# A second Strassen level for the products 0 and 1 of seven convolution pairs, with h's quarter sums prepared in v's stage

## The chip, the cores and the metric

The kernel runs on one core of a Trainium2 chip. A core has TensorE (matrix products; PE in the profile, and PEld for its weight loads), VectorE (DVE), ScalarE (ACT), GpSimd (POOL) and SyncE (SP, which here issues almost all DMAs). The metric is the device time of one execution in microseconds, the median of several runs.

## What is computed

One layer of a decoder trunk over 1024 positions of width 1024, in float32. After a norm, h is multiplied by one wide weight matrix, and the columns feed a gated linear attention and a short gated convolution; the two are merged, projected, gated once more and normed.

```python
h = rms_norm(x, norm_mix_g[i])
proj = jnp.einsum('bsd,dc->bsc', h, w_in[i])
(q, k, v, z_a, gk_low, cb, cc, xc, z_c, g_a, g_c) = jnp.split(proj, idx, axis=-1)
...
u = causal_dwconv(cc * xc, conv_w[i])
y_c = jnp.einsum('bsc,cd->bsd', (cb * u) * jax.nn.silu(z_c), w_branch_c[i])
```

`causal_dwconv` adds, for every channel, the values of a position and of the two before it, each times its own weight. The change lies in the four products cb, cc, xc and z_c (1024 columns each) and in this convolution.

## The kernel before

**Products.** Every matrix is cut into halves in both directions, and each product of 2x2 blocks is done by Strassen's scheme with seven block products instead of eight, numbered 0 to 6. Both operands of each are sums of blocks. A float32 value is split into a high part that the fast matmul form takes and a low part with the rest (`split`: a cast on ScalarE, a subtraction on VectorE), and a product is three matmuls: high x high, high x low, low x high (`mm3`). h's seven operands, high and low, are resident (`hres`). The weights' operands are made as they are needed in a ring of eight buffers (`RING`, tags whi and wlo): a load into raw, a sum into T, the split.

**Cells.** A `Cell` makes 256 columns of one projection for all positions: seven products of twelve matmuls of 512 columns each. Its partial results lie in three PSUM banks X, Y and V: product 0 goes to X and is copied to Y, product 1 to V, 2 adds onto Y, 3 onto X, 5 onto V, 4 and 6 onto Y. As soon as a quarter of the result is there, the cell's `cons` reads it from the bank. Two cells run in step as a pair (`pairs`), with the banks of one set each; the next pair uses the same six banks. In the convolution there are eight pairs, in this order: cc0 with xc0, zc0 with cb0, cc1 with xc1, and so on to zc3 with cb3. Four further cells, q0, k0, q1 and k1, run alone before them, and the gate cells (ga, gc) and the attention after them. v and z_a come first of all, by a function of their own (`wide`).

**Second level.** `Deep` takes product 0 of both cells of a pair, which have h's block in common, and does it again by Strassen's scheme: seven products of half size in both directions, 42 matmuls of 256 columns in place of 24 of 512. It runs in four steps (`run`, k from 0 to 3) that `line_up` puts between the last products of the pair before. Two more PSUM buffers (tag o: w and u) hold its partial results; ScalarE copies them on (into u, into the bank, and d into SBUF), and VectorE writes b's bank as u + d. Its h operands are quarter blocks of `hres[0]` and four sums of them, which `quarters` makes on VectorE during the first convolution pairs (t1 to t4; one of them overwrites a quarter of h itself, once product 0 of the second pair is done). In the kernel before, the six pairs from cc1 on have it.

**Order.** Nothing is issued as it is written. `Flow` records each operation, works out due times backwards from the order of the main matmuls, which is fixed, and then plans all five queues by a table of costs: of the operations that could start on an engine, the one that is due first. `nc.hurry` makes an operation due earlier by so many microseconds. `weave` spreads a generator's pieces over the ticks that the products give (two a product, one for each product of a second level). The engines then run the planned order as it stands.

**The convolution.** cc's results are copied into t (both halves of the positions, 1026 columns with two zeros ahead), xc's multiply them, and once both halves are there, three operations of 1024 columns make u. zc's sigmoid and product and then cb's results multiply u, half by half, and u is stored.

**Beside it.** `weights` prepares sums of blocks of the two last weight matrices for later (loads into wt, subtractions, stores to wtd), in eight pieces of 1 MB. The mask trim, the scratch tile junk and the identity are kept in SBUF from start to end.

Of the kernel before, what the change touches and what calls it, by code (L numbers as in the profile page):

```python
# [9 lines left out]
F32 = mybir.dt.float32  # L10
# [509 lines left out]
def kernel(  # L520
# [37 lines left out]
    ident = cp.tile([P, P], F32, name="ident")  # L558
    make_identity(tc.nc, ident.place())
    mhalf = cp.tile([P, 1], F32, name="mhalf")  # L560
    nc.gpsimd.memset(mhalf, -0.5)
    trim = cp.tile([P, P], I32, name="trim")
# [3 lines left out]
    junk = cp.tile([P, 512], BF16, name="junk")  # L566
# [11 lines left out]

    ped = [dram(f"ped{b}", D) for b in range(8)]
# [106 lines left out]
    def ring_steps(name, side, raw, fresh, mixed):  # L686
# [21 lines left out]
        if side == "A":  # L708
            a11, a21, a12, a22 = (r(n) for n in range(4))

            def s1():
# [3 lines left out]
                for kt in range(4):  # L715
# [5 lines left out]
                    lambda: put(a22())]  # L721
        b11, b12, b22, b21 = (r(n) for n in range(4))
        return [lambda: put(b11()), lambda: two("T1", b12, b11), lambda: two("T2", b22, k("T1")),
                lambda: put(b21()), lambda: two("T3", b22, b12), lambda: put(b22()),
                lambda: two("T4", b21, k("T2"), over="T2")]
# [5 lines left out]
    class Cell:  # L731
# [3 lines left out]
        def __init__(self, name, side, src, res, cons, prods=ORDER, begin=None, s1=None, u2=None, s5=None, fresh=(), mixed=False):  # L735
            self.name, self.side, self.src, self.res, self.cons = name, side, src, res, cons
            self.prods, self.begin, self.after = list(prods), begin, None
            self.get = {"u2": u2, "s5": s5}
            self.s1, self.seed, self.ready, self.halves = s1, None, lambda k: True, None
            self.raw, self.ring, self.order, self.Y, self.deep = [None] * 4, {}, None, None, None  # L740
            self.steps, self.fresh = ring_steps(name, side, self.raw, fresh, mixed), fresh
# [92 lines left out]
    class Deep:  # L834


        def __init__(self, pair, turned, pool):
            self.pair, self.turned, self.pool, self.ring = pair, turned, pool, []
            for c in pair:
                c.deep, c.prods = self, [k for k in c.prods if k]  # L840

        slots = 4
# [4 lines left out]
        def load(self, k):  # L847
            for c in self.pair:
                c.load(0)

        def prep(self, k):
# [3 lines left out]
            a, b = (c.raw[0] for c in self.pair)  # L855
            name = self.pair[0].name + self.pair[1].name
# [29 lines left out]
        def run(self, k):  # L886
            self.prep(k)
            a, b = self.pair
            left, right = slice(0, 256), slice(256, 512)
            if k == 0:  # L890
# [3 lines left out]
                self.u = pso.tile([P, 512], F32, tag="o", name=f"{a.name}u", bufs=2)  # L894
                a.X = bank(a, 0)
                nc.scalar.copy(self.u[:, left], self.w[:, left])
                nc.scalar.copy(a.X[:, left], self.w[:, left])
                self.d = self.pool.tile([P, 256], F32, tag="dw", name=f"{a.name}dw")
                nc.scalar.copy(self.d, self.w[:, right])
            elif k == 1:  # L900
                self.product(2, self.u[:, left], False)
                nc.scalar.copy(self.u[:, right], self.u[:, left])
                self.product(3, a.X[:, left], False)
            elif k == 2:
                self.product(4, self.u[:, right], False)
                nc.scalar.copy(a.X[:, right], self.u[:, right])
                b.X = bank(b, 0)
                tt(b.X.rearrange("p (n c) -> p n c", n=2), self.u.rearrange("p (n c) -> p n c", n=2),
                   self.d[:, None, :].to_broadcast([P, 2, 256]), op=ALU.add)
            else:  # L910
                self.product(5, a.X[:, right], False)
                self.product(6, b.X[:, left], False)
# [129 lines left out]
    with phase("prep0") as pool:  # L1042
        pr_ = slot(4, "h", "pTraw", (2, SEQ), F32)
# [31 lines left out]
        load(trim, tri)  # L1075
# [198 lines left out]
    with phase("v", [ph["prep0"]]) as qp:  # L1274
# [72 lines left out]
        weave(decays(0), 2)  # L1347
# [12 lines left out]
    with phase("qk", [ph["v"]]) as qp:  # L1360
# [65 lines left out]
        for g in range(4):  # L1426
            t, u = [], []

            def cc_begin(g=g, t=t, u=u):
                for j in range(2):  # L1430
                    t.append(vp.tile([P, SEQ + 2], F32, tag=f"t{j}", name=f"t{g}_{j}"))
                    u.append(vp.tile([P, SEQ], F32, tag=f"u{j}", name=f"u{g}_{j}"))
                    nc.gpsimd.memset(t[j][:, 0:2], 0.0)

            def cc_cons(i, j, src, t=t):
                nc.scalar.copy(t[j][:, 2 + i * HALF:2 + (i + 1) * HALF], src)

            done = {0: 0, 1: 0}

            def xc_cons(i, j, src, g=g, t=t, u=u, done=done):  # L1440
                ts = t[j][:, 2 + i * HALF:2 + (i + 1) * HALF]
                tt(ts, src, ts, op=ALU.mult)
                done[j] += 1
                if done[j] == 2:
                    k = 2 * g + j
                    nc.vector.tensor_scalar(u[j], t[j][:, 0:SEQ], cw[:, 0, k:k + 1], None, op0=ALU.mult)
                    stt(u[j], t[j][:, 1:SEQ + 1], cw[:, 1, k:k + 1], u[j], op0=ALU.mult, op1=ALU.add)
                    stt(u[j], t[j][:, 2:SEQ + 2], cw[:, 2, k:k + 1], u[j], op0=ALU.mult, op1=ALU.add)

            def zc_cons(i, j, src, g=g, u=u):  # L1450
                s = ev(f"s{g}_{i}_{j}")
                us = u[j][:, i * HALF:(i + 1) * HALF]
# [4 lines left out]
            def cb_cons(i, j, src, g=g, u=u):  # L1457
                k = 2 * g + j
                us = u[j][:, i * HALF:(i + 1) * HALF]
                tt(us, src, us, op=ALU.mult)  # L1460
                store(ud[i][k // 4][:, k % 4, :], us)

            for m, cons in (("cc", cc_cons), ("xc", xc_cons), ("zc", zc_cons), ("cb", cb_cons)):
                convs.append(Cell(f"{m}{g}", "B", W[f"{m}{g}"], hres, cons, begin=cc_begin if m == "cc" else None))
# [4 lines left out]
    with vp:  # L1469
        def weights(vp):  # L1470


            for w in range(2):
                for kt in range(4):
                    t = vp.tile([P, 4, 512], F32, tag="wt", name=f"wt{w}_{kt}", bufs=1)
                    load(t, wb[w][:, :, kt, :].rearrange("n p c -> p n c"))
                    yield 14
                    b11, b12, b22, b21 = (t[:, n] for n in range(4))
                    if w:
                        for n, q in enumerate((b11, b12, b22, b21)):  # L1480
                            k = kt + 4 * (n >= 2)
                            act(q, q, AF.Copy, scale=gple[:, k:k + 1])
                            if n != 1:
                                store(wtd[w][4 + (n + 1) // 2][:, kt, :], q)
                    tt(b11, b12, b11, op=ALU.subtract)
                    yield 2
                    tt(b12, b22, b12, op=ALU.subtract)
                    yield 2
                    tt(b22, b22, b11, op=ALU.subtract)
                    yield 2  # L1490
                    tt(b21, b21, b22, op=ALU.subtract)
                    for n, q in enumerate((b11, b22, b12, b21)):
                        store(wtd[w][n][:, kt, :], q)
                    yield 4
# [510 lines left out]
```

## Time and profile before

| | |
|---|---|
| median of 3 runs | 1077.94 us (1077.93 to 1078.25) |
| profiled execution | 1077.08 us, of which the span is 1075.3 us |
| granted TensorE clock | 0.998 of full speed |
| convolution stage (first cc0 matmul to the last cb3 one) | 311 to some 614 us |
| HBM | 158 MB read, 81 MB written, 222 GB/s over the span |

All instructions show the line of the planner's `emit` (L508), so the rows are told apart by tiles: cc1V is bank V of cell cc1, cc1w and cc1u are the second level's own buffers, cc1xc1S is a sum for it, turnedh one of h's quarter sums. Buffer numbers are left out. A row of the chain of waits is the time in which TensorE worked on that tile; x12 is one product of 512 columns.

### The profile page before, as it was taken

Reading aid. Unit: us, or ns where it says so; the run is one execution under the profiler, and the core shown is the slowest. Engines: PE = TensorE matmul, PEld = TensorE weight load, DVE = VectorE, ACT = ScalarE, POOL = GpSimd, SP = SyncE. Lnnn points to the kernel's source line nnn. Section 1 sums busy time; section 2 is a strip of 40 time slices with the busy share of each in tenths; the row PEclk is TensorE's granted clock in tenths of the full one; section 3 lists DMA queues with packets and bytes.
Section 4 is the critical chain, followed back from the end, with each engine's and each line's share of the span. In section 5 each row is a group of like instructions: output and inputs, shape, how many; then the busy total and the mean of one; then the engine's idle time right before and its main releaser. Section 6 shows DMA issues by size and latency. Waiting matters only on the chain.

```text
span 1075.3 us, 15008 instructions
## 1 busy us (share of the span) xinstructions
PE 1066.0 (99%) x4989; PEld 892.8 (83%) x4989; DVE 897.1 (83%) x1417; ACT 624.8 (58%) x1143; POOL 45.6 (4%) x83
## 2 busy tenths in 40 slices
PE   9999999999999999999999999999999999999997
PEld 7888888888888888888888888888888888888886
DVE  6998567679999787979868788887999978889896
ACT  6778538756544444555344366666756635466555
POOL 0000000000000000000000011110000000011021
PEclk9999999999999999999999999999999999999999
DMA  9963564467762445555324679979586879799963
GB/s 326 361 229 120 168 210 138 148 205 232 238 215 100 151 171 167 205 187 176 123 84 142 213 245 328 329 272 332 196 309 214 289 217 303 236 343 337 303 226 139
DMA packets 144830, 239.98 MB, mean 223 GB/s; under 512 B 12016, under 2 KB 57328, under 8 KB 141808
## 3 DMA queue, kind: packets, MB, share of 16 engines
q1 hardware_dynamic: 144608, 238.76, 65.7%
q8 instruction: 39, 0.64, 0.2%
q14 instruction: 39, 0.32, 0.1%
q10 hardware_dynamic: 144, 0.26, 0.1%
HBM read 158.24 MB, written 80.74 MB: 222 GB/s over the span
## 4 chain that ended last, share of the span: by engine, by line
PE 99%; DVE 0%; ACT 0%; issue 0%; POOL 0%; DVEq 0%; ACTq 0%
PE vY L508 3%; PE zaY L508 3%; PE pe L508 2%; PE vX L508 2%; PE zaX L508 2%; PE zaV L508 2%; PE vV L508 2%; PE op L508 2%; PE kv L508 1%; PE ga1Y L508 1%; PE ga3Y L508 1%; PE cb1Y L508 1%; PE xc2Y L508 1%; PE xc1Y L508 1%; PE cb0Y L508 1%; PE xc3Y L508 1%
## 5 line engine op out<-in xcount | busy, mean ns | idle before, releaser
L508 ACT ACT_TABLE_LOAD x22 | 28.2, 1283 | 1.1 <-PEq L1994 0.7
L508 ACT ACTIVATE junk<-x 128x512 bf16<-128x512 f32 (+1 forms) x30 | 18.0, 600 | 12.2 <-DVE x L508 11.8
L508 DVE TENSOR_TENSOR wt<-wt 128x512 f32<-128x512 f32 x32 | 22.0, 689 | 0.2
L508 DVE SCALAR_TENSOR_TENSOR u<-t,vec,u 128x1024 f32<-128x1024 f32 x16 | 20.2, 1282 | 0.1
L508 POOL MEMSET t<- 128x2 f32 x8 | 0.8, 99 | 441.8 <-PE k1Y L508 241.6
L508 POOL TENSOR_SCALAR rg<-ms 128x1 f32<-128x1 f32 x8 | 6.4, 797 | 262.5 <-ACT junk L508 262.3
L508 DVE SCALAR_TENSOR_TENSOR S<-S,dds,kv 128x256 f32<-128x256 f32 x24 | 10.4, 477 | 5.4 <-PE kv L508 5.4
L508 ACT CAST S<-S 128x512 fp32r<-128x512 f32 x14 | 8.7, 619 | 10.4 <-PE op L508 9.5
L508 ACT ACTIVATE junk<-op 128x256 bf16<-128x256 f32 x32 | 12.1, 379 | 3.0 <-PE op L508 2.9
L508 ACT ACTIVATE og<-op,or 128x256 f32<-128x256 f32 x32 | 13.3, 468 | 0.9 <-POOL or L508 0.9
L508 ACT ACTIVATE oq<-oq,vec 128x512 f32<-128x512 f32 x20 | 13.2, 715 | 0.0
L508 PE MATMUL op<-v,aTh 128*128 128x256 f32 x64 | 12.8, 283 | 0.0
L508 PE MATMUL pe<-wpehi,pTlo 128*128 128x512 f32 x32 | 12.7, 397 | 0.0
L508 PE MATMUL pe<-wpehi,pThi 128*128 128x512 f32 x32 | 12.6, 393 | 0.0
L508 PE MATMUL pe<-wpelo,pThi 128*128 128x512 f32 x32 | 12.6, 393 | 0.0
L508 DVE TENSOR_TENSOR szl<-og,szl 128x512 f32<-128x512 f32 x16 | 11.0, 687 | 1.6 <-ACT og L508 1.6
L508 POOL TENSOR_TENSOR or<-or,mhalf 128x2 f32<-128x2 f32 x16 | 11.8, 738 | 1.3
L508 DVE SCALAR_TENSOR_TENSOR hq<-hq,vec,rt 128x512 f32<-128x512 f32 x16 | 11.2, 744 | 0.6 <-PE rt L508 0.6
L508 DVE TENSOR_TENSOR x<-x,pe 128x512 f32<-128x512 f32 (+1 forms) x18 | 11.2, 631 | 0.3
L508 DVE STREAM_TRANSPOSE oT<-szl 128x512 f32<-128x512 f32 x16 | 11.3, 706 | 0.1
L508 DVE TENSOR_TENSOR u<-u,s 128x512 f32<-128x512 f32 x16 | 11.0, 689 | 0.3
L508 POOL TENSOR_SCALAR or<-oms 128x2 f32<-128x2 f32 x16 | 5.8, 363 | 124.9 <-ACT junk L508 124.9
(3184 smaller groups left out, 4202.6 us busy)
## 6 DMA issues: line engine op xcount, KB each, us to landing
wtd<-wt SPq DMA_DIRECT2D x44, 256.0 KB, 2.5
wt<-in_wb_dram SPq DMA_DIRECT2D x8, 1024.0 KB, 5.1
v<-vd SPq DMA_DIRECT2D x16, 512.0 KB, 6.1
wgq<-wtd SPq DMA_DIRECT2D x7, 1024.0 KB, 7.5
qk<-qkd SPq DMA_DIRECT2D x12, 512.0 KB, 6.2
vraw<-in_wv_dram SPq DMA_DIRECT2D x20, 256.0 KB, 4.1
zaraw<-in_wv_dram SPq DMA_DIRECT2D x20, 256.0 KB, 4.0
uq<-ud SPq DMA_DIRECT2D x5, 1024.0 KB, 6.2
```

Source lines behind the costliest of these rows:

```text
L508: o.call(*[place(a) for a in o.args], **{k: place(a) for k, a in o.kw.items()})
```

## The change

- The second level is given to products 0 and 1 of the seven pairs from zc0 on. A pair's first `Deep` (product 0) starts five products before the end of the pair ahead instead of three; its second (product 1) starts with the pair itself, one step ahead of each of the first four products. That one first copies X to Y, and its results are bank V. Its weight operands are the sums T1 of both cells.
- The quarter sums of `hres[0]` and `hres[1]`, eight with their high and low parts, are made in v's stage (`quarter_sums`), stored to DRAM (tqd), and loaded again when the convolution's memory is there (`quarters`).
- The convolution works on halves of the positions: t has 514 columns, the two last columns of the first half are kept in end, u has 512, is stored to DRAM (yd) and loaded again (y, one buffer) by zc's `cons`.
- `weights` works in sixteen pieces of half the columns, with its operations due 60 us earlier.
- trim and junk are made in the attention's memory, and junk again for the last stages; the identity lies in the first stage's memory. This and the two points before leave room for the second set of quarter sums.

```diff
+            t = keep["T1"] = bp.tile([P, 4, P], F32, tag="T", name=f"{name}T1", bufs=4)
+            tt(t, b12(), b11(), op=ALU.subtract)
...
-            a, b = (c.raw[0] for c in self.pair)
+            a, b = (c.operand(self.k) for c in self.pair)
...
             if k == 0:
-                self.w = pso.tile([P, 512], F32, tag="o", name=f"{a.name}w", bufs=2)
+                for c in self.pair if self.k else ():
+                    c.Y = bank(c, 1)
+                    nc.scalar.copy(c.Y, c.X)
+                self.w = pso.tile([P, 512], F32, tag="o", name=f"{name}w", bufs=2)
...
-                for c in self.pair:
-                    c.Y = bank(c, 1)
-                    nc.scalar.copy(c.Y, c.X)
+                for c, t in ((a, self.a), (b, self.b)):
+                    if self.k:
+                        c.V = t
+                        c.c22 = c.taken("s5", t)
+                    else:
+                        c.X = t
...
+            own = [(g[s], k) for s, k in (g[0].order or [(s, k) for k in g[0].prods for s in range(len(g))])]
             if g[0].deep:
                 for n in range(4):
-                    todo.insert(len(todo) - 3 + n, (g[0].deep, n))
-            todo += [(g[s], k) for s, k in (g[0].order or [(s, k) for k in g[0].prods for s in range(len(g))])]
+                    todo.insert(len(todo) - 5 + n, (g[0].deep[0], n))
+                    own.insert(2 * n, (g[0].deep[1], n))
+            todo += own
...
+        def quarter_sums(k):
...
+            def apart(n, a, b):
+                t, o = tile(n), tile("o")
+                tt(t, at(hi, *a), at(hi, *b), op=ALU.subtract)
+                tt(o, at(lo, *a), at(lo, *b), op=ALU.subtract)
+                tt(t, t, o, op=ALU.add)
+                return t
...
+            def put(n, src):
+                hl = [qp.tile([P, 512], F32, tag="t1", name=f"qs{k}{n}{w}", bufs=3).rearrange("p (a b) -> p a b", a=2) for w in "hl"]
+                split(*(t.bitcast(F32R) for t in hl), src)
+                for w, t in enumerate(hl):
+                    store(tqd[k][n][w], t)
...
+            def cc_cons(i, j, src, g=g, rows_of=rows_of, ends=ends):
+                t = rows_of[i, j] = vp.tile([P, HALF + 2], F32, tag="t", name=f"t{g}_{i}_{j}", bufs=2)
+                if i:
+                    nc.scalar.copy(t[:, 0:2], ends.pop(j))
+                else:
+                    nc.gpsimd.memset(t[:, 0:2], 0.0)
+                nc.scalar.copy(t[:, 2:], src)
...
+                nc.vector.tensor_scalar(u, t[:, 0:HALF], cw[:, 0, k:k + 1], None, op0=ALU.mult)
+                stt(u, t[:, 1:HALF + 1], cw[:, 1, k:k + 1], u, op0=ALU.mult, op1=ALU.add)
+                stt(u, t[:, 2:], cw[:, 2, k:k + 1], u, op0=ALU.mult, op1=ALU.add)
+                store(yd[k][i], u)
+
+            def zc_cons(i, j, src, g=g, gated=gated):
+                k = 2 * g + j
+                y = vp.tile([P, HALF], F32, tag="y", name=f"y{k}_{i}")
+                load(y, yd[k][i])
+                s = gated[i, j] = ev(f"s{g}_{i}_{j}")
                 act(s, src, AF.Sigmoid)
                 tt(s, src, s, op=ALU.mult)
-                tt(us, us, s, op=ALU.mult)
...
+                tt(s, y, s, op=ALU.mult)
...
+                    for cs in (slice(0, 256), slice(256, 512)):
+                        t = vp.tile([P, 4, 256], F32, tag="wt", name=f"wt{w}_{kt}_{cs.start}")
+                        soon(load, t, wb[w][:, :, kt, cs].rearrange("n p c -> p n c"))
+                        yield 7
...
+            for n in range(4):
+                while n == 3 and not k and convs[0][-1].Y is None:
+                    yield 1
+                for t, src in zip(back[n], tqd[k][n]):
+                    load(f(t), src)
                 yield 1
...
-        for g in convs[2:]:
-            Deep(g, turned, vp)
+        for k in range(2):
+            for g in convs[1:]:
+                Deep(g, k, turned[k], vp)
+            weave(quarters(k), 1)
         weave(weights(vp), 10)
-        weave(quarters(turned), 20)
```

In v's stage, VectorE's order now has rows such as these between the weights' low parts (qs0 and qs1 are quarter sums of h's operands 0 and 1, o the scratch tile, vT and v6 v's own weights):

```order
L508 TENSOR_TENSOR qs_1450<-h1hi 128x512
L508 TENSOR_TENSOR v6lo_1457<-vT_989,v6hi_1444 128x512
L508 TENSOR_TENSOR qs1o<-h1lo 128x512
L508 TENSOR_TENSOR qs_1450<-qs_1450,qs1o 128x512
L508 TENSOR_TENSOR qs03l<-qs_1399,qs03h 128x512
L508 TENSOR_TENSOR v6lo_1479<-vT_995,v6hi_1469 128x512
```

Before, the corresponding rows stood in direct succession:

```order
L508 TENSOR_TENSOR v6lo_1420<-vT_993,v6hi_1416 128x512
L508 TENSOR_TENSOR v6lo_1436<-vT_999,v6hi_1432 128x512
L508 TENSOR_TENSOR v6lo_1452<-vT_1017,v6hi_1448 128x512
L508 TENSOR_TENSOR vu_1379<-vV_1181,vu_1379 128x512
L508 TENSOR_TENSOR vu_1386<-vV_1188,vu_1386 128x512
```

So four quarter-sum operations now stand between two weights' low parts of v's last product.

At the change from the pair cc1/xc1 to zc1/cb1, ScalarE's order before, around the first step of zc1's second level (zc1w its first results, u and dw its copies, zc1X the bank):

```order
L508 COPY zc1u<-zc1w 128x256
L508 COPY zc1X<-zc1w 128x256
L508 COPY zc1dw<-zc1w 128x256
L508 CAST cb1hi<-cb1T_4095 128x512
L508 COPY zc1u<-zc1u 128x256
```

and after, around the first step of the level on product 1 (zc11w), with the reading of cc1's last Y (into t) and both copies of X to Y ahead of it:

```order
L508 COPY t_1_0_4500<-cc1Y 128x512
L508 COPY zc1Y<-zc1X 128x512
L508 CAST cb1hi<-cb1raw_4329 128x512
L508 COPY cb1Y<-cb1X 128x512
L508 COPY zc11u<-zc11w 128x256
L508 COPY zc1V<-zc11w 128x256
L508 COPY zc11dw<-zc11w 128x256
```

The copies for product 1's second level stand behind the copy of the b-cell's Y.

More of the change, by code (lines that the diff above doesn't have):

```diff
@@ L848, in load @@
             for c in self.pair:
[L849 removed]
+                c.load(self.k)
         def prep(self, k):
@@ L1470, in weights, with soon @@
         def weights(vp):
+            def soon(do, *a, **kw):
+                nc.hurry = 60.0
+                do(*a, **kw)
+                nc.hurry = 0.0
             for w in range(2):
                 for kt in range(4):
[L1475 to L1484, printed above, removed]
@@ L1661 @@
     with phase("att", [ph["conv"]]) as ap:
+        trim = ap.tile([P, P], I32, name="trim")
+        junk = ap.tile([P, 512], BF16, name="junk")
+        load(trim, tri)
         aTf = [ap.tile([P, 2, P], F32, name=f"aT{i}") for i in range(2)]
```

190 lines of the change are left out of this document (97 added, 93 removed).

## The prediction

> **What bounds the kernel now.** I read the page's totals and its chain of waits first, then TensorE's own waits, then the chain through the convolution stage, and last the busy time of the other engines there.
>
> ```profile
> span 1075.3 us, 15008 instructions
> ...
> PE 1066.0 (99%) x4989; PEld 892.8 (83%) x4989; DVE 897.1 (83%) x1417; ACT 624.8 (58%) x1143; POOL 45.6 (4%) x83
> ...
> PE 99%; DVE 0%; ACT 0%; issue 0%; POOL 0%; DVEq 0%; ACTq 0%
> ```
>
> The chain is 99% TensorE. TensorE's waits are one row, before the first warming matmul:
>
> ```profile
> PE warm L508 <- DVE zero L508: 1.4, 1, 1.4
> ```
>
> So between that and its last matmul TensorE never stands still: the time is the sum of its matmuls, and every other engine only has to stay ahead of it. An edit can then do two things: change that sum, or make TensorE wait. Here is the chain in a group of two cells without a second level, and in the next group, which has one for its first product (names ending in w and u, and the x6 pieces):
>
> ```profile
> 311.41 2.72 PE cc0X L508 x12
> ...
> 349.49 2.72 PE zc0X L508 x12
> ```
>
> ```profile
> 379.41 1.42 PE cc1w L508 x12
> 380.83 2.75 PE cb0Y L508 x12
> 383.58 0.71 PE cc1u L508 x6
> 384.29 0.71 PE cc1X L508 x6
> 385.00 2.75 PE zc0Y L508 x12
> 387.75 0.71 PE cc1u L508 x6
> 388.45 2.75 PE cb0Y L508 x12
> 391.20 0.71 PE cc1X L508 x6
> 391.91 0.72 PE xc1X L508 x6
> 392.63 2.75 PE cc1V L508 x12
> ...
> 430.37 2.75 PE zc1V L508 x12
> ```
>
> A plain group takes 349.49 - 311.41 = 38.08 us, fourteen products of 2.72. A group with a second level takes 430.37 - 392.63 = 37.74. One second level therefore saves 0.34 us. From its parts: it is 42 matmuls of 256 columns, 1.42 + 5 x 0.71 and 0.01 = 4.98, and the four products that follow a piece of it take 2.75 instead of 2.72, 0.12 more: 5.10 against 2 x 2.72 = 5.44.
>
> **The change part by part. TensorE.** Before, six pairs of cells have a second level, each for product 0. After, seven pairs (all but the first) have it for products 0 and 1: fourteen, eight more. In the built order TensorE has 4958 rows instead of 4814, 144 more, which is 8 x (42 - 24), so the change does what it says. The sum: 8 x 0.34 = 2.7 us less. The upper bound, if the pieces hand over without the 0.03, is 8 x (5.44 - 4.98) = 3.7; I take 2.7, which is what whole groups showed. The profiled execution took 1077.08 us around its span of 1075.3; it would come to 1074.4. The median of the runs, 1077.94, lies 0.86 above it, and becomes 1075.2.
>
> A rule that speaks against it is weighed here, and nothing later rests on it. A weight load lasts this long:
>
> ```profile
> L508 PEld LDWEIGHTS cb1X<-h0hi,zc1cb1Bhi x2: 192/192/192, 429.4 to 429.7; 128*128 128x128 f32 x2
> ```
>
> The Trainium skill (TensorE: Matmul & The Clock Gate, Back-to-back issue gap) says that the spacing of matmuls in a stream is set by the load and the matmul together, so halving the columns halves only one of them. Were the load the limit at 0.19 us, a second level would take 42 x 0.19 = 8.0 us instead of 5.44 and eight would cost 20 us: 1098. The rows above give 1.42 us for twelve such pairs, 0.118 each, so here the loads are hidden and the trace decides for 2.7 less.
>
> **VectorE in v's stage.** The quarter sums are 28 subtractions and additions of 128x512 there, and 14 fewer in the convolution. What one costs is the distance of starts in the DVE's timeline, not the length of a row, since rows overlap:
>
> ```profile
> 423.91 0.42 DVE L508 TENSOR_TENSOR cc2xc2S<-cc2raw,xc2raw 128x256 f32<-128x256 f32 x1
> 424.25 0.68 DVE L508 TENSOR_TENSOR zc1T<-zc1raw,zc1T 128x512 f32<-128x512 f32 x1
> 424.85 0.75 DVE L508 TENSOR_SCALAR u<-t,vec 128x1024 f32<-128x1024 f32 x1
> 425.63 1.28 DVE L508 SCALAR_TENSOR_TENSOR u<-t,vec,u 128x1024 f32<-128x1024 f32 x1
> 426.83 0.68 DVE L508 TENSOR_TENSOR cb1lo<-cb1T,cb1hi 128x512 fp32r<-128x512 f32 x1
> 427.43 0.69 DVE L508 TENSOR_TENSOR cb1X<-zc1u,zc1dw 128x512 f32<-128x512 f32 x1
> ```
>
> 0.60 us for 512 columns (424.25 to 424.85), 0.34 for 256, 1.20 for the 1024-wide fused operation. The 28 take 16.8 us. By the order they begin after the first of v's weights for product 5; the room from there is in the first of these windows (PE, PEld, DVE, ACT, POOL, clock, DMA share, GB/s):
>
> ```profile
> 110.60:157.90 47.30, 47.30 (x210) 38.87 (x209) 27.48 (x42) 21.10 (x36) 0.00 (x0) 1.00 0.53 172
> 235.10:311.20 76.10, 76.10 (x337) 63.04 (x336) 69.04 (x133) 45.72 (x91) 0.00 (x0) 1.00 0.78 236
> 311.20:349.30 38.10, 38.10 (x169) 31.54 (x169) 36.01 (x58) 16.80 (x30) 0.20 (x2) 1.00 0.41 132
> 349.30:606.00 256.70, 256.70 (x1252) 216.92 (x1251) 207.14 (x328) 119.84 (x223) 1.15 (x8) 1.00 0.46 158
> ```
>
> 47.3 - 27.5 = 19.8 us free, so they fit, and a weight delayed behind one has this lead:
>
> ```profile
> L508 PE MATMUL vY<-v6lo,h6hi x16: 389/389/389, 147.2 to 157.4; 128*128 128x512 f32 x16
> L508 DVE TENSOR_TENSOR v6lo<-vT,v6hi x4: 685/692/693, 124.9 to 134.0; 128x512 fp32r<-128x512 f32 x4
> ```
>
> Written at 124.9, used at 147.2: 22 us. Cost nothing; without that cover it would be up to 16.8. ScalarE adds eight casts, some 5 us, to 21.1 of 47.3; the sixteen 256 KB stores add 4.2 MB to 172 GB/s x 47 us = 8 MB.
>
> **VectorE in the convolution.** Each additional second level costs it four 256-wide sums (1.36), one and a half more low parts (0.94) and the 512-wide b = u + d (0.60): 2.9 us, x8 = 23. The weights' 32 subtractions become 64 of 256: 64 x 0.34 - 32 x 0.60 = +2.6. The convolution by halves turns 16 fused operations of 1024 into 32 of 512; not shown, bounded by 0.60 (half of 1.20) and 0.75 (the row of 1024 scalars), so 0 to +4.8, taken +2. Removed: 14 x 0.60 = 8.4. Net +19 (17 to 22). The stage (the last two windows) had 243 us busy in 295; it gets 262 in 292, 90%. The q/k stage runs at 69.0 in 76.1, 91%, with no TensorE wait, so 90% alone is no bound, but the slack per group falls from 6 us to under 4.
>
> **The hand-overs that get shorter.** A second level uses a bank of TensorE's output that another engine has to fill in time. Two places decide. First, its last piece adds onto b = u + d: in the rows above, DVE wrote cb1X at 427.43, 0.69 long, and TensorE begins that piece at 429.5:
>
> ```profile
> L508 PE MATMUL cb1X<-h0hi,zc1cb1Bhi x2: 283/283/283, 429.5 to 429.8; 128*128 128x256 f32 x2
> ```
>
> 1.4 us spare. This place occurred six times and now fourteen. Second, Y. Before, the products 1 of both cells ran between the previous pair's last product and the next Y. Now only one 12-matmul piece does. After the previous a-cell's product 6 there remain 2.72 + 1.42 = 4.1 us, in which the old Y is read and the new one copied, by copies such as this:
>
> ```profile
> 430.09 0.58 ACT L508 COPY zc1Y<-zc1X 128x512 f32<-128x512 f32 x1
> ```
>
> ScalarE's order there is the last one shown with the change. Now the copies that the second level waits for stand behind cb1Y, which waits for VectorE's reading of the old bank. After a cc pair the a-cell's way is two copies, 1.2 us plus hand-overs of some 0.3: 2.5 spare. After a zc pair it is sigmoid, product on VectorE and copy, 0.6 + 0.7 + 0.6 and hand-overs: about 1.7 spare. I take nothing, covered by these spares; a VectorE that runs more than 1.7 us late there ends the cover, in up to seven groups.
>
> **Loads.** Fourteen of the sixteen 256 KB reloads of h's sums stand in SP's order behind the last q/k store, which in the trace went out just ahead of the first weight load:
>
> ```profile
> 322.91 0.38 SPq L508 DMA_DIRECT2D wt<-in_wb_dram  x1
> ...
> wtd<-wt SPq DMA_DIRECT2D x44, 256.0 KB, 2.5
> wt<-in_wb_dram SPq DMA_DIRECT2D x8, 1024.0 KB, 5.1
> ```
>
> A megabyte lands in 5.1 us, so the fourteen and half a megabyte of weights between them take some 21 us: the pair for the first new piece (TensorE at 336) is there by 326, the next four by 333 (used from 341), the last by 344; product 1's are used from 354. Ten us spare. The y reloads go through one buffer, between two reads 2.75 + 0.71 + 2.75 + 1.43 = 7.6 us apart; they take 2.5 to 5.1, so 2.5 us are spare. The weights come as sixteen pieces of half the size through one buffer, with the same bytes; trim is one 64 KB load at the attention's start, and the pieces that need the masked scores stand 41 matmuls, 9 us, behind the first scores. I take nothing for each; one that comes late costs TensorE a few us once, and a late y holds VectorE, which leads to rival 3.
>
> **Rivals.**
> 1. Forecast: only the sum changes, waits under 0.5 us: 1074.4 to 1075.8. Chance 0.54. For it: no wait in 1075 us and VectorE at 91% elsewhere.
> 2. A few scattered waits of 0.6 to 4 us in the fourteen bank hand-overs or at a late reload: 1075.8 to 1080. Chance 0.22. For it: spares of 1.4 to 1.7 us; against: the six old ones never waited.
> 3. Slower: the Y bank. VectorE, 90% full, reaches the old Y more than 1.7 us late, ScalarE stands at the b-cell's Y copy and the second level's copies behind it are late too. From 0.4 us of wait a group the gain is gone; at 1.2 us in seven groups it is 8.4 - 2.7: 1083.6. Chance 0.23. Beside it: the Trainium skill (TensorE: Matmul & The Clock Gate, Architectural detail) has ACT and DVE as strict first-in-first-out; ScalarE's row at 430.09 stands where its planned order has it, between two casts, so the trace agrees.
> 4. The weight load bounds the additional pieces: 1098. Chance 0.01, by the 0.118 us above.
>
> **Numbers.** Likeliest 1075.2, its own range 1074.2 to 1075.8. The whole range goes up to 1083.5, which leaves out some 0.15 above. About 0.2% (2.2 us) is what a measurement of this kernel can tell from no change. Faster by more: all of the first case and the lower edge of the second (up to 1075.8), 0.55. Within: the rest of the second and the slower side's start, 0.21. Slower: 0.24.
>
> **What would show it.** Right: groups of 37.4 us in the chain (fourteen 2.72, less 2 x 0.34), TensorE's waits still a single row, VectorE near 262 us in the convolution. Wrong: rows of TensorE waiting for ScalarE's or VectorE's writes of Y, V or u; pieces of 256 columns slower than 0.12; waits for turned, y or trim.

## The result and the profile after

The changed kernel takes 1076.10 us (median of 20 runs, 1075.34 to 1077.16) against 1077.79 for the kernel before (20 runs): a ratio of 0.9984, with a 95% interval of 0.9978 to 0.9991, so 1.7 us less (1.0 to 2.4). Timed once more in the experiments it was 1075.84 against 1077.32, 0.9985 (0.9976 to 0.9994). It is faster, and by less than the 0.2% that the prediction set as its bound. 2.7 us had been predicted. A kernel for which no interval is given below was executed once; of such kernels the stage, the pieces and the waits are compared, not the time.

The page's totals and the sum of the chain of waits of the changed kernel, with its share by engine:

```profile
span 1073.9 us, 15781 instructions
...
PE 1064.2 (99%) x5133; PEld 896.6 (83%) x5133; DVE 929.7 (87%) x1543; ACT 651.6 (61%) x1235; POOL 45.8 (4%) x83
...
PE 98%; ACT 0%; DVE 0%; DMA 0%; POOL 0%; issue 0%; DVEq 0%; ACTq 0%
```

VectorE has 33 us more to do than before (897.1), ScalarE 27, and the chain is still 98% TensorE. TensorE's waits are the old one, and a short one at the start, which the second profile of the same kernel doesn't have:

```profile
PE warm L508 <- DVE zero L508: 1.4, 1, 1.4
PE pe L508 <- ACT pThi L508: 0.3, 1, 0.3
```

One group of the chain of waits with a second level for both products (cc10 and zc10 are levels on product 0, cc11 and zc11 on product 1; start, us, piece):

```profile
392.76 1.43 PE cc11w L508 x12
394.19 2.77 PE cc1Y L508 x12
396.95 0.71 PE cc11u L508 x6
...
411.49 1.43 PE zc10w L508 x12
412.92 2.75 PE xc1V L508 x12
415.67 0.72 PE zc10u L508 x6
...
430.24 1.43 PE zc11w L508 x12
```

From one level's start to the same place in the next group are 430.24 - 392.76 = 37.48 us. Before it was 37.74, and 37.4 were predicted. The pieces are a hair longer than those of before: 1.43 instead of 1.42, 0.72 where it was 0.71, 2.77 and 2.76 instead of 2.75.

The whole stage runs from the first row of cc0X to the first row of ga0V in the same view, after and before:

```profile
312.05 2.72 PE cc0X L508 x12
...
613.10 2.72 PE ga0V L508 x12
```

```profile
614.71 2.72 PE ga0V L508 x12
```

That is 301.05 us after; before, with its first cc0X at 311.41, 303.30. The stage saved **2.25 us**. Some of it was lost ahead of the stage: cc0X begins 0.64 us later. The span fell by 1.4, from 1075.3 to 1073.9.

Busy time in the windows of the prediction, after (PE, PEld, DVE, ACT, POOL, clock, DMA share, GB/s):

```profile
110.60:157.90 47.30, 47.30 (x209) 38.75 (x208) 43.29 (x68) 24.35 (x43) 0.00 (x0) 1.00 0.74 251
...
311.20:349.30 38.10, 38.10 (x188) 32.26 (x187) 29.92 (x53) 17.59 (x37) 0.20 (x2) 1.00 0.76 252
349.30:606.00 256.70, 256.70 (x1389) 222.35 (x1388) 230.30 (x432) 142.48 (x303) 1.16 (x8) 1.00 0.59 190
```

VectorE in v's last product went from 27.5 us to 43.3 (44.3 by the prediction's sum), in the convolution from 243 to 260 (262 predicted), and TensorE is busy in every microsecond of both.

The hand-over that rival 3 fears, after the pair zc1/cb1. ScalarE's and VectorE's timelines after (start, us), and the first matmul that adds onto the new Y (ns of one, first and last start):

```profile
465.38 0.59 ACT L508 ACTIVATE s<-zc1Y 128x512 f32<-128x512 f32 x1
466.98 0.57 ACT L508 COPY cc2Y<-cc2X 128x512 f32<-128x512 f32 x1 [1.01 <-DVE s L508]
...
468.85 0.57 ACT L508 COPY xc2Y<-xc2X 128x512 f32<-128x512 f32 x1 [0.64 <-DVE s L508]
```

```profile
466.26 0.68 DVE L508 TENSOR_TENSOR s<-zc1Y,s 128x512 f32<-128x512 f32 x1
```

```profile
L508 PE MATMUL cc2Y<-h2hi,cc2hi x4: 387/389/394, 469.0 to 471.1; 128*128 128x512 f32 x4
```

The copy ends at 466.98 + 0.57 = 467.55 and the bank is needed at 469.0: 1.45 us spare, where 1.7 were worked out. The b-cell's copy, xc2Y, begins 1.3 us after that, but its first product starts only at 473.2.

### The profile page after: what moved, and what is told of

Its sections match the earlier page's. It is cut to its first block, busy times and chain, and to the rows that moved or that the text cites. A ratio compares the mean times of both kernels' runs of the same rounds, so it can differ in the third digit from the quotient of the medians.

```text
span 1073.9 us, 15781 instructions
## 1 busy us (share of the span) xinstructions
PE 1064.2 (99%) x5133; PEld 896.6 (83%) x5133; DVE 929.7 (87%) x1543; ACT 651.6 (61%) x1235; POOL 45.8 (4%) x83
## 4 chain that ended last, share of the span: by engine, by line
PE 98%; ACT 0%; DVE 0%; DMA 0%; POOL 0%; issue 0%; DVEq 0%; ACTq 0%
PE vY L508 3%; PE zaY L508 3%; PE pe L508 2%; PE vX L508 2%; PE zaX L508 2%; PE zaV L508 2%; PE vV L508 2%; PE op L508 2%; PE kv L508 1%; PE cc1Y L508 1%; PE zc2Y L508 1%; PE zc0Y L508 1%; PE cc3Y L508 1%; PE cc2Y L508 1%; PE zc1Y L508 1%; PE ga1Y L508 1%
## 5 line engine op out<-in xcount | busy, mean ns | idle before, releaser
L508 DVE TENSOR_TENSOR wt<-wt 128x256 f32<-128x256 f32 x64 | 26.7, 418 | 0.1
L508 DVE SCALAR_TENSOR_TENSOR u<-t,vec,u 128x512 f32<-128x512 f32 x32 | 23.7, 745 | 0.1
L508 ACT ACTIVATE wt<-wt,vec 128x256 f32<-128x256 f32 x32 | 13.7, 499 | 0.0
L508 DVE TENSOR_TENSOR s<-y,s 128x512 f32<-128x512 f32 x16 | 11.0, 685 | 0.1
```

Source lines behind the costliest of these rows:

```text
L508: o.call(*[place(a) for a in o.args], **{k: place(a) for k, a in o.kw.items()})
```

## Experiments

In each table or sentence below the stage is the one from the first cc0X to the first ga0V, read as above. A level's price is read from the starts of TensorE's matmuls in the trace, in ns: its six pieces, and what the products of 512 columns behind them take beyond 2720.

### Both kernels once more

No edit; only the profiles were wanted.

> The kernel before, once more, for the start. In the two profiles TensorE's first ga0p product began at 28.93 us before and 29.36 after, and the whole first 50 us ended 0.49 us later after the change. Theory A (the moved identity, junk and mask trim change the start): this profile shows the start of before again, ga0pX at 28.9 within 0.1, and cc0X at 311.2. Rival B (the start varies from execution to execution with the arrival of the first loads): ga0pX moves by 0.2 us or more from 28.93. Either way the convolution, first cc0X to first ga0V, lasts 303.30 us within 0.1, as its pieces repeat to a nanosecond within one profile.

> The changed kernel, once more. Theory A (the start is the change's own): ga0pX at 29.36 within 0.1 again, cc0X at 311.9. Rival B (it varies): ga0pX anywhere between 28.9 and 29.5, and other than 29.36 by over 0.1. The convolution, first cc0X to first ga0V, lasts 301.05 us within 0.1 by both.

The stage repeated: 303.30 and 301.07 us. The start did not. The first ga0pX came at 29.21 in the kernel before (28.93 in its first profile) and at 29.04 in the changed one (29.36). The 0.43 us by which the first pair of profiles differed there is within what one kernel does by itself, so this pair can't be read as a loss by the change; theory A falls in its sharp form. Between v's first matmul and z_a's first, 84.89 and 84.92 us passed before, 85.04 and 85.01 after: this part of the loss, some 0.1 us, repeats, and did so in all twelve profiles with the change (84.99 to 85.04). Which of the new operations in v's stage costs it was not tried.

### The second level for product 0 alone

```diff
-            for g in convs[1:]:
+            for g in convs[1:] if k == 0 else ():
                 Deep(g, k, turned[k], vp)
...
-                    todo.insert(len(todo) - 5 + n, (g[0].deep[0], n))
-                    own.insert(2 * n, (g[0].deep[1], n))
+                    todo.insert(len(todo) - 3 + n, (g[0].deep[0], n))
...
                     else:
                         c.X = t
+                        c.Y = bank(c, 1)
+                        nc.scalar.copy(c.Y, c.X)
```

> The changed kernel with the second level for product 0 of the seven pairs alone; product 1 is one plain product of each cell again. The quarter sums in v's stage, their reloads (h1's too, which nothing reads here), the convolution by halves and the weights in sixteen pieces stay. Seven levels instead of six before and fourteen after. Theory 1 (each level saves what whole groups of before showed, 0.34 us, and the preparation costs nothing in the convolution): first cc0X to first ga0V lasts 303.30 - 0.34 = 302.96 us. Theory 2 (a level costs more with the new preparation, since in the trace after its pieces of six matmuls take 716 ns instead of 711 and the pieces of twelve 1428 instead of 1421, and saves 0.31): the same pieces are slow here as well and the convolution lasts 303.30 + 2.04 - 7 x 0.31 = 303.2. Theory 3 (only two levels a group slow each other's pieces): pieces of 711 and 1421 here, 302.96. The time: 0.3 us under before, plus up to 0.6 if the start and v's end cost that with the change.

The stage lasts from 311.96 to 615.31, 303.35 us, 0.05 longer than before though one level was added. The pieces are the slow ones of the changed kernel: 1428, 724, 711, 724, 712 and 720 ns in every one of the seven levels, 41 more than the 4978 of before. Theory 2 is right in kind, and its size was too small: with what the next products lose, a level on product 0 saves 294 ns here and 346 before. The time, 1077.88 us, is 1.0004 of before (0.9994 to 1.0013): no difference. So nearly all that the change gained in this stage, 303.35 - 301.05 = 2.30 us, are the seven levels on product 1, and the old six became dearer by nearly what the added seventh saves.

### Where the second level's operands lie

Product 0's pieces that read the reloaded sums (turned) had become slower, alike in every group, and those on h's own quarters hardly. In the built programs before and after, these tiles lie at other places in SBUF: before, both begin at byte 32 of a 64-byte line; after, turned0's high part and turned1's low part begin at byte 0. Four kernels move tiles and compute the same.

align32 pads t and joins turned1's parts:

```diff
-t = rows_of[i, j] = vp.tile([P, HALF + 2], F32, tag="t", name=f"t{g}_{i}_{j}", bufs=2)
+t = rows_of[i, j] = vp.tile([P, HALF + 16], F32, tag="t", name=f"t{g}_{i}_{j}", bufs=2)[:, 0:HALF + 2]
...
-th, tl = (vp.tile([P, 4, 2, 256], F32R, name=f"turned{k}{w}") for w in "hl")
+both = vp.tile([P, 8, 2, 256], F32R, name=f"turned{k}hl")
+th, tl = both[:, 0:4], both[:, 4:8]
```

> The changed kernel with two tiles padded: t is allocated with 528 columns (514 used), and turned1's high and low parts lie in one tile. Nothing computed changes. In the built program of before both turned tiles begin at byte 32 of a 64-byte line; after the change turned0's high part and turned1's low part begin at byte 0, the others at 32; here all four begin at byte 32 again. In the trace the pieces of six matmuls that read a turned tile took 706 ns before and 724 (product 0) or 711 (product 1) after, the same in every group. Theory P (the place of the turned tiles in memory sets this): product 0's pieces on turned tiles go from 724 to about 707, its twelve from 1428 to 1421, product 1's from 711 to about 707, and the convolution, first cc0X to first ga0V, from 301.05 us to 300.5 (14 x 0.04 less). Rival (the place has nothing to do with it; it is the order of the pieces or the work beside them): 724, 711 and 301.05 again. The time: 0 to 0.5 us under the changed kernel, 1.7 to 2.2 under the kernel before.

gap64 lays the convolution's tiles out by hand, where its memory is opened (a tile that is used later under the same tag takes this place; high0 has the two 32-byte pads ahead of the high parts instead):

```diff
+            if self.name == "conv":
+                self.real.tile([P, 1536], F32R, tag="turned0h_0", name="at_turned0h", bufs=1)
+                self.real.tile([P, 514], F32, tag="t_0", name="at_t_0", bufs=1)
+                self.real.tile([P, 8], F32, tag="pad0", name="at_pad0", bufs=1)
+                self.real.tile([P, 1536], F32R, tag="turned0l_0", name="at_turned0l", bufs=1)
...
+                self.real.tile([P, 2048], F32R, tag="turned1h_0", name="at_turned1h", bufs=1)
+                self.real.tile([P, 2], F32, tag="end_1", name="at_end_1", bufs=1)
+                self.real.tile([P, 8], F32, tag="pad1", name="at_pad1", bufs=1)
+                self.real.tile([P, 2048], F32R, tag="turned1l_0", name="at_turned1l", bufs=1)
```

> The changed kernel with the convolution's tiles laid out by hand: all four turned tiles at byte 32 of a 64-byte line, and the low part of each 8256 bytes behind the high part (in the run align32 turned0 had 8256 and turned1 8192). Nothing computed changes. What one second level saved against 5.44 us, its pieces and the slower products behind them counted, in medians of the traces: 346 ns before; 293 for product 0 and 308 for product 1 after; 406 and 320 in align32. Theory P1 (the distance of high and low part matters besides the 64-byte place): product 1 saves about 406 ns too, and the convolution, 300.20 us in align32, lasts 299.6. Rival P2 (only the 64-byte place matters, and product 1's rest lies in hres[1]): product 1 stays at 320 and the convolution at 300.2. In both the time is under the changed kernel's by 0.8 to 1.5 us.

shift32 moves all of SBUF's tiles up by 32 bytes:

```diff
-    mhalf = cp.tile([P, 1], F32, name="mhalf")
+    mhalf = cp.tile([P, 9], F32, name="mhalf")[:, 0:1]
```

> The changed kernel with everything in SBUF moved up by 32 bytes: h's parts and the ring of weights begin at byte 0 of a 64-byte line instead of 32, turned0's high part at 32 instead of 0, turned1's high part at 0 instead of 32. Nothing computed changes. Theory A (byte 32 is the quick place by itself): product 0's pieces on turned tiles go from 724 to 707 ns, product 1's from 711 to 724, and the pieces on h's own quarters (712) and perhaps the plain products (2.720 us) become slower. Theory R (what counts is whether the high part lies as the weights do): product 0's stay at 724, product 1's at 711 or 707, and nothing else moves. Neither (it is the distance between tiles): all as in the changed kernel, since no distance changes.

> As gap64, with the two high parts of the turned tiles alone moved up by 32 bytes, from byte 32 of a 64-byte line to byte 0; the low parts, the weights and h's parts stay at byte 32. shift32 left two readings: theory R (a high part that does not lie on the same byte of its 64-byte line as the weights and the low part is slow) expects product 0's six-matmul pieces on turned tiles to go from 707 ns back to about 724, product 1's from 706 to 711 to 724 and the convolution from 300.61 us (gap64) up by 0.2 to 0.6. Rival D (large distances between tiles decide, 32 bytes do nothing) expects 707, 706 and 300.6 again.

What was measured (byte: where in its 64-byte line each tile begins; h and weights: where h's parts and the ring of weights begin; saved: medians over the levels, in ns; the row of fill2 is that of an experiment below, whose added operations changed the order in which tiles were placed):

| kernel | h and weights | turned0 high, low | product 0: a piece on turned, saved | turned1 high, low | product 1: a piece on turned, saved | stage, us |
|---|---|---|---|---|---|---|
| before | 32 | 32, 32 | 707, 346 | none | none | 303.30 |
| after | 32 | 0, 32 | 724, 293 | 32, 0 | 711, 308 | 301.05 |
| shift32 | 0 | 32, 0 | 724, 294 | 0, 32 | 711, 306 | 301.08 |
| align32 | 32 | 32, 32 | 707, 406 | 32, 32 | 712, 320 | 300.19 |
| fill2 | 32 | 32, 32 | 707, 400 | 32, 0 | 711, 306 | 300.40 |
| gap64 | 32 | 32, 32 | 707, 346 | 32, 32 | 706, 320 | 300.61 |
| high0 | 32 | 0, 32 | 724, 294 | 0, 32 | 705, 387 | 300.52 |

The chain of waits shows the same in coarser steps. A piece of product 0 and the group's two ends in align32:

```profile
392.03 1.43 PE cc11w L508 x12
...
414.89 0.71 PE zc10u L508 x6
...
429.39 1.43 PE zc11w L508 x12
```

and in high0:

```profile
392.75 1.42 PE cc11w L522 x12
...
415.58 0.72 PE zc10u L522 x6
...
430.15 1.42 PE zc11w L522 x12
```

The piece zc10u is 0.72 in the changed kernel and in high0 and 0.71 in align32; the groups take 37.48, 37.40 and 37.36 us.

What follows. Theory P of align32, that the place in memory sets the pieces, is borne out for product 0, whose pieces went from 724 to 707 there, but not for product 1 (712 instead of the 707 expected); the stage gained more than its 0.55 us, since the products behind the pieces gained too. For product 0 the reverse was seen as well: 707 became 724 when high0 moved the high part by 32 bytes and nothing else of product 0's operands. Byte 32 is not quick by itself: in shift32 every tile moved by 32 bytes and no piece changed, so theory A falls. Theory R, that the high part has to lie in its line as the weights do, fits every row of product 0. It does not fit product 1, where the same move of 32 bytes made a level cheaper (320 to 387 saved). P1, the 8256 bytes between high and low part, falls too: product 1 stayed at 320 in gap64. And with both its tiles at byte 32 product 0 saved 346 in two kernels and 400 to 406 in two others; there the pieces differ little (4978 and 4977 ns in gap64 and align32), and the products behind them lose 116 ns or 57. So neither P1 nor P2 foretold gap64's stage of 300.61, and the place of these operands is worth up to 0.11 us a level, some 0.9 us in fourteen.

The table counts bytes in lines of 64 and so hides a difference that the built programs show. Counted in lines of 128 bytes and from the byte at which the weights begin, turned0's high part begins at 0 in before and gap64 (346 saved), at 32 in after, shift32 and high0 (293, 294), and at 64 in align32 and fill2 (406, 400): one price for each place, with the low part at 64 in all of them but align32. turned1's high part too has one price for each place, in another order: 0 in align32 and gap64 (320), 32 in high0 (387), 64 in after, shift32 and fill2 (306 to 308). This was read off afterwards and no kernel was made to test it; why the two products differ stays open.

align32 and gap64 are also the fastest of the kernels that were executed more than once: 1074.96 us, 0.9977 of before (0.9968 to 0.9987), and 1075.02, 0.9979 (0.9970 to 0.9988). The changed kernel was timed beside gap64:

> The changed kernel as it is, timed beside gap64 on the same chip: 1.7 us under the kernel before within 0.7, the convolution 301.05 us within 0.1, the start anywhere from 28.9 to 30.0 us at ga0pX, as in the eight profiles so far of either kernel.

Its 1075.84 and 0.9985 (0.9976 to 0.9994) overlap with both, so the times alone don't separate them; the stage, which repeats to 0.02 us in three profiles of the changed kernel (301.05, 301.07 and 301.08), does. The last profile's start was at 29.73, still later than the others of this kernel. No version combined align32's place for product 0 with high0's for product 1.

### Does the Y bank decide?

path4 and path2 put four or two copies in the way in which zc's Y becomes free:

```diff
                 act(s, src, AF.Sigmoid)
+                for _ in range(4):
+                    nc.scalar.copy(s, s)
                 tt(s, src, s, op=ALU.mult)
```

> The changed kernel with four extra copies of s onto itself on ScalarE, between zc's sigmoid and VectorE's product that reads the bank: they lengthen the way in which the old Y bank becomes free after a zc pair by four starts of about 0.55, some 2.2 us, and leave VectorE's work as it is. In the trace after, zc1's last Y was read until 466.94, the copy cc2Y ended at 467.55 and its first matmul began at 469.0: 1.5 us spare. Theory 1 (the hand-over of Y decides from 1.5 us on): TensorE waits about 0.7 us for cc1Y, cc2Y and cc3Y, three rows of waits that were not there, 2 us in all, and the time is 2 us above the changed kernel. Rival (more is spare, since the first products of the next group need the bank later, or ScalarE reorders round it): no such rows, same time within 0.3. Rival 3 of the prediction (the copies behind it on ScalarE become late too): waits for the second level's u as well, over 1.2 us a group.

> As path4 with two copies in place of four, about 1.1 us on the way in which zc's old Y becomes free (path4 showed TensorE waiting 1.8, 2.0 and 1.4 us for cc1Y, cc2Y and cc3Y). If the spare is the 1.5 us read between the end of copy cc2Y (467.55) and its first matmul (469.0), there is no wait, or under 0.3 us each where another operation comes between. If the spare is less than read, each of the three waits by 0.5 us or more.

TensorE's waits in path4 (us in total, times, longest):

```profile
PE cc2Y L508 <- ACT cc2Y L508: 2.0, 1, 2.0
PE cc1Y L508 <- ACT cc1Y L508: 1.8, 1, 1.8
...
PE cc3Y L508 <- ACT cc3Y L508: 1.4, 1, 1.4
PE ga1Y L508 <- ACT ga1Y L508: 0.4, 1, 0.4
```

The three rows are those that theory 1 named, with 5.2 us instead of 2; the stage lasts 307.07, 6.0 longer than the changed kernel's, and the span is 7.3 longer. No row names the second level's u, which rival 3 had expected. The way grew by more than the copies, because ScalarE puts a cast between them and VectorE's product waits its turn. In path2 one wait row stands, 0.3 us for cc2Y, and the stage is 301.83, 0.8 longer. By the starts of the matmuls the group with cc2 lost 0.6 us, that with cc3 0.3, and that with cc1 nothing. Its chain shows the way through the hand-over step by step:

```profile
465.17 2.51 PE cb1Y L508 x11
467.68 0.02 issue
467.70 0.63 ACT xc2hi L508
468.33 0.68 DVE s L508
469.01 0.02 issue
469.04 0.58 ACT cc2Y L508
469.62 0.04 issue
469.66 3.03 PE cc2Y L508 x12
```

TensorE starts on cc2Y 0.04 us after the copy ends. The chain names the cast xc2hi ahead of VectorE's reading, but in the built program that reading waits only for the second extra copy, done at 466.27 + 1.28 = 467.55. ScalarE's and VectorE's timelines of path2 show what came between:

```profile
465.27 0.59 ACT L508 ACTIVATE s<-zc1Y 128x512 f32<-128x512 f32 x1
465.76 0.61 ACT L508 CAST cc2hi<-cc2raw 128x512 fp32r<-128x512 f32 x1
466.27 1.28 ACT L508 COPY s<-s 128x512 f32<-128x512 f32 x2
```

```profile
467.72 0.68 DVE L508 TENSOR_TENSOR s<-cb1u,s 128x512 f32<-128x512 f32 x1
468.32 0.68 DVE L508 TENSOR_TENSOR s<-zc1Y,s 128x512 f32<-128x512 f32 x1
```

Another cast, cc2hi, stands between the sigmoid and the copies, and another product of VectorE ahead of its reading of the bank. So the copy cc2Y ends at 469.62 instead of 467.55, 2.07 us later. Less the spare of 1.45 that leaves 0.6, which is what the group lost. Rival 3's place was real, and the spare as small as read.

### How full may VectorE be?

```diff
                 tt(s, y, s, op=ALU.mult)
+                for _ in range(2):
+                    tt(s, s, s, op=ALU.max)
```

(four in fill4)

> The changed kernel with 32 more operations of 128x512 on VectorE in the convolution (s = max(s, s) twice after each of zc's products, behind the reading of the bank): 32 x 0.60 = 19 us, so VectorE goes from 265 us of the stage's 301 to 284, 94%. Theory 1 (the hand-overs have the spares of 1.4 to 1.7 us and the planner keeps the urgent ones first): no new wait of TensorE, the stage stays 301.05 within 0.2. Rival 3 (VectorE's fullness makes Y, V or u late): rows of TensorE waiting for ScalarE's or VectorE's writes of them, the stage 2 us longer or more.

> As fill2 with 64 more operations, 38 us: VectorE would have 303 us of work in a stage of 301. Theory 1 (VectorE decides only when it is full): TensorE waits by a few us, mostly near the stage's end, since work can be put off into the next stage; 2 to 6 us more. Rival 3 (latency at the hand-overs decides long before): 10 us or more, spread over all the groups.

Busy time over the changed kernel's 301.05 us of the stage, first of the changed kernel, then of fill2 and fill4 (the same window: PE, PEld, DVE, ACT):

```profile
311.89:612.94 301.05, 301.05 (x1602) 259.78 (x1601) 265.18 (x491) 162.31 (x342) 1.36 (x10) 1.00 0.62 201
```

```profile
311.89:612.94 301.05, 301.05 (x1605) 260.01 (x1604) 279.90 (x520) 162.59 (x343) 1.41 (x10) 1.00 0.62 200
```

```profile
311.89:612.94 301.05, 296.10 (x1577) 255.04 (x1576) 287.14 (x534) 158.44 (x339) 1.42 (x10) 1.00 0.60 195
```

fill2 has VectorE at 279.9 us, 93%, with no wait of TensorE; the window holds 29 operations more, not 32. Its stage is shorter than the changed kernel's (300.40), since its tiles lie at other bytes. fill4 asks for more than there is, and TensorE waits:

```profile
PE xc3Y L508 <- ACT xc3Y L508: 2.2, 1, 2.2
...
PE xc1Y L508 <- ACT xc1Y L508: 1.1, 1, 1.1
PE xc2Y L508 <- ACT xc2Y L508: 1.1, 1, 1.1
PE xc2V L508 <- DVE xc2lo L508: 0.6, 1, 0.6
```

Its stage, 306.51, is 6.1 us longer than that of fill2, whose tiles begin at the same bytes: just past theory 1's 2 to 6 us, and the waits are spread over three groups, not gathered near the end. Three of the four come where rival 3 put them, at the copies of Y behind a zc pair, but only with VectorE past 93%. The changed kernel's 88% of the stage leaves room for 15 us more.

## Why the prediction was right, and what was off

**The number.** 1075.2 was predicted and 1076.10 measured. That is 0.3 above the likeliest case's own range, and it lies in the whole range only because this went up to 1083.5 for rivals that did not happen. A gain of more than 0.2% had a chance of 0.55 and did not come; what came, less than that, had 0.21. Of the signs of being wrong one came by a hair: pieces of 724 ns are 0.1207 a matmul, above 0.12. So the mechanism was right, and the size, 2.7 us where 1.7 came, was not.

**TensorE's sum decides.** Right. No wait came with the change beyond 0.3 us at the start, and the stage's 2.25 us are the matmuls' own.

**0.34 us a level, eight of them.** The mechanism held and the size was off. The term 8 x 0.34 took the price of the old six levels for the new ones and left the old ones as they were. In the changed kernel a level saves 293 (product 0) and 308 ns (product 1), so seven of each save 4.2 us where six had saved 2.1 in the traces: 2.1 by these medians, 2.25 by the stage, instead of 2.7. The six old levels became dearer by 0.05 each, which the prediction had no term for. That this comes with the operands' place in memory is shown for product 0 (align32, high0); the move was a by-product of the halved rows and the second set of sums. Had they lain as in align32, the stage would have saved 3.1 us, more than predicted.

**What the stage doesn't explain.** The median fell by 1.7, the stage by 2.25, and v's stage lost 0.1: 0.4 us are left. Half of it repeats at the very end, a term that the prediction didn't have. From the first matmul of gt0X to the end of the span 84.46 and 84.48 us passed before, and 84.63 to 84.94 in the twelve profiles with the change. TensorE's last matmul ends 76.62 us after that first one in all of them, and the last packet of the last store at 83.14 in the first profile before and after; what follows it there are SyncE's closing waits for the DMA queues. What made them longer was not tried. About 0.2 us remain, and 0 to 0.5 in the other kernels with an interval (prod0, align32, gap64 and the changed kernel's second timing). TensorE's first ga0pX, which closes the start, came at 28.93 and 29.21 in two profiles before and between 28.94 and 30.01 in twelve with the change, 29.40 in the mean. Each kernel scatters by as much as the difference, so that the start became later by some 0.3 us is possible and not shown: it would take more profiles of the kernel before, and a kernel with the identity and the junk tile put back, which was not tried.

**VectorE.** The sums were right, 43.3 us against 44.3 in v's last product and 260 against 262 in the convolution, and so was that they hide from TensorE's waits: fill2 shows that some 15 us more would hide too. (The order shown with the change has three quarter-sum operations between two of v's low parts, not four.)

**The hand-overs.** The spare after a zc pair was 1.45 us, worked out as 1.7; after b = u + d it was 1.5 (VectorE writes xc2X until 459.93, the piece on it begins at 461.4), worked out as 1.4. They cost nothing, and path2 and path4 show that this hung on about a microsecond.

**Loads.** None was waited for. The pair of loads for the first new piece was issued at 326.1 and 326.6 and took 4.3 us, so it was there by 330.9 instead of 326; the first matmul on it began at 337.1, six us later, where ten had been counted on.

**The rivals.** Rival 2 (scattered waits, 1075.8 to 1080): the median of 1076.10 lies in its range, yet the mechanism is not there, since no hand-over and no reload was late. Rival 3 (slower by the Y bank): it did not happen, and its place, the copies of Y, is where waits appear first, both when the way is lengthened (path2) and when VectorE is filled (fill4). Rival 4 (weight loads at 0.19 us each): a piece of twelve takes 1.43 us after, 0.119 a matmul, so it falls. The Trainium skill (TensorE: Matmul & The Clock Gate, Back-to-back issue gap) says that the load and the matmul together set the spacing; here the loads of 0.19 us don't become the limit. The 512-column products behind a level's pieces lose 57 to 147 ns; whether that is the loads' is not shown.

## What to carry to other kernels

Where one engine's sum is the time, predict a repeated saving from the kernel as it will be: a change that moves tiles in SBUF can move the price of matmuls that it doesn't touch, here by 0.05 us in 5.4, and with a gain of 0.3 each this counts. Compare the same matmuls in the two traces by the distance of their starts; when they differ alike in every group, move a tile by 32 bytes before looking for waits. And a spare of one and a half microseconds at a bank is safe only until one more operation is planned between: in path2 a cast on ScalarE and a product on VectorE.

## What was not expected of the hardware

Two kernels that give TensorE the same matmuls in the same order, with operands 32 bytes apart in SBUF, differ by 2.4% in some pieces (high0 and gap64: 724 and 707 ns for six matmuls of 256 columns), within a nanosecond or two alike in every group; moving everything by 32 bytes (shift32) changes nothing. After a run of 256-column matmuls the products of 512 columns are slow for a while: in the changed kernel the first three take 232 to 233 ns each in the mean and only the tenth is back at 227; in align32 the sixth is.
